# A hybrid SSD and attention block on one core: operands at equal offsets, a later residual, and a head in an order set by hand

## The chip, the cores and the metric

The kernel runs on one core of one Trainium2 chip. The metric is the time of one execution on the device, in microseconds. The core's engines are named as in the profile: PE (matrix products; PEld is its loading of the stationary operand), DVE (vector), ACT (scalar), POOL (general), SP (here the engine whose queue issues the DMAs). SBUF is the on-chip memory with 128 partitions, and PSUM holds the sums of products.

## The reference, cut to what matters

```python
D_MODEL, SEQ, D_FF = 1024, 512, 2816      # one layer, batch 1, float32
def reference(x, ln_in_g, ln_in_b, w_in, ...):
    h = _layernorm(x, ln_in_g, ln_in_b)   # (x - mean) * rsqrt(var + eps) * g + b
    mix = _mixing(h, w_in, ...)           # h @ w_in, cut into the inputs of two branches:
                                          #  SSD (32 heads, chunked scan; y + xs * D_skip),
                                          #  indexer + attention (16 heads over chosen keys),
                                          #  two gates; w_br_ssd, w_br_att, then w_out
    h = _layernorm(DN_ALPHA * h + mix, ln1_g, ln1_b)
    f = _conv_ffn(h, ffn_w_up, ffn_conv_w, ffn_conv_b, ffn_w_down)
    return _layernorm(DN_ALPHA * h + f, ln2_g, ln2_b)
```

What matters here is the first line (the normalized input, called the **head** of the kernel with the first small projections), and that h comes back later as the residual `DN_ALPHA * h`.

## The kernel before, in words

Nearly every product is made in three parts: a float32 matrix is split into a high part (`hi`, a copy rounded by ACT) and a low part (`lo`, the difference, by DVE), and PE adds hi·hi, lo·hi and hi·lo into one PSUM tile (`mm3`, `proj`, `tok_mm`). A weight tile of 128 x 1024 numbers is loaded by SP into a raw buffer `wraw` (pool `wrw`, two buffers), split into `whi` and `wlo` (pool `whl`, three buffers each), and used by 24 products of 128 x 128 by 512 columns (384 for the indexer's queries `w_qi`). `wload` issues these loads ahead of their use, but SP's queue is in order: a load that waits for a raw buffer holds back what stands behind it.

The head: x is loaded as four tiles of 128 tokens. DVE makes mean and variance (`ln_stats`), POOL the inverse root (a power, line 155), and x is normalized in place (tile 1 by ACT, the others by DVE, line 295). PE transposes the tiles into PSUM (line 311), DVE or ACT scales each of the 8 transposed blocks by g and b into `hf` (lines 315 and 317, g and b in the table `pvec`), ACT and DVE split it into `hhi` and `hlo` (`split`). PE then projects `w_small` (104 columns per block of 128 rows), `w_qi[0]` to `w_qi[3]`, and the first large one is `w_ckv`. Meanwhile POOL makes the low parts of the first two weight tiles (line 303) and multiplies the normalized x by g and adds b for the residual, 16 operations of 128 x 512 (lines 327 and 328, g and b spread over the partitions in `gB` and `bB`); the result goes to DRAM (`htok_d`, line 330) and is read back late (line 906). `prow` is a table of row vectors spread over the partitions. `Dv` holds the SSD's D_skip, 64 x 16 numbers for each half of the partitions, loaded by two DMAs at line 482.

After the head come the xbc and z projections and the scan, `w_br_ssd`, the attention heads one by one (`tm` is the mask with the position bias, made by POOL at line 763 and read by DVE at line 774, then the key-value products), `w_br_att`, `w_out`, the second normalization, `w_up` and `w_down`. PE runs in one order written out by the program in the middle part; elsewhere a scheduler decides by priorities.

SBUF tiles come from two sides: pools of weights, `hhi`/`hlo` and others from the left, and the pool `wk` (activations, gates, keys and so on) from the right. In the built program the left tiles that PE reads begin at 128 modulo 512 bytes, those of the right at 480, and `ckhi`/`cklo` at 160, because the small tile `m8` of 32 bytes lies ahead of them. An operand of the right beside one of the left thus begins 32 bytes off, modulo 64. In the program 1057 of the 4053 products of 512 columns have a stationary and a moving operand that differ in this way: all those of `w_br_ssd` (384, names `yhi`, `ylo`), of `w_br_att` (192, `yahi`, `yalo`), and of `w_down` and `w_out` where one operand is of the right, besides the keys' and values' from `ckn`.

Of the kernel before, what the change touches and what calls it, by code (L numbers as in the profile page):

```python
# [67 lines left out]
def block_kernel(ctx, tc, A, out):  # L68
# [215 lines left out]
    raws = [wrw.tile([P, D], F32, name="wraw", tag="wraw") for _ in range(2)]
    nc.sync.dma_start(raws[0][:, :KD * 104], A["w_small"])
    nc.sync.dma_start(raws[1], A["w_qi"][0])
    stats = [ln_stats(t, i) for i, t in enumerate(xt)]
    for i, (t, (mv, rs)) in enumerate(zip(xt, stats)):
        if i == 1:
            nm = st([P, 1], "nm")  # L290
            nc.vector.tensor_scalar(nm, mv[:, 0:1], -1.0, None, OP.mult)
            nc.scalar.activation(t, t, AF.Identity, bias=nm)
            nc.scalar.activation(t, t, AF.Copy, scale=rs)
        else:
            nc.vector.tensor_scalar(t, t, mv[:, 0:1], rs, OP.subtract, OP.mult)
# [810 lines left out]
```

## Time and profile before

| what | us |
|---|---|
| median of three runs | 1142.55 (1140.33 to 1143.06) |
| the profiled execution's own time | 1140.93 |
| its span, from the first to the last instruction | 1139.2 |
| PE busy | 1104.3 |
| DVE, ACT, POOL busy | 806.7, 442.8, 184.3 |

The profile is of one execution. An engine's busy time is to be set against the span; what an idle stretch of PE ended with, and in which stretch it lies, is read from the waits, the windows and the timelines below. The granted clock is the share of TensorE's 2.4 GHz that the throttle let through: 1.00 is 2.4 GHz, 0.50 is 1.2 GHz.

### The profile page before, as it was taken

What the parts mean: (1) busy time and instruction counts of PE and PEld (TensorE: products, weight loads), DVE (VectorE), ACT (ScalarE), POOL (GpSimd) and SP (SyncE); (2) the same over time, 40 slices, a digit from 0 to 9 for tenths busy, and PEclk for the clock granted to TensorE, in tenths of its full rate; (3) what the DMA queues carried; (4) which work ended last, traced back from release to release, by engine and by line L of the source; (5) the groups of instructions that cost most, each with busy time, mean ns of one, the idle gap of its engine ahead of it and who ended that gap; (6) DMA issues with size and microseconds to landing.
All of it is one profiled execution on the core that took longest, in us unless ns stands there. A gap on an engine that the chain in (4) does not pass through costs nothing.

```text
span 1139.2 us, 14494 instructions
## 1 busy us (share of the span) xinstructions
PE 1104.3 (97%) x5394; PEld 902.7 (79%) x5394; DVE 806.7 (71%) x1536; ACT 442.8 (39%) x694; POOL 184.3 (16%) x179
## 2 busy tenths in 40 slices
PE   4799999999999999999999999999999999999996
PEld 3688888887888888878778778889888888888885
DVE  7479798876789899958998936586665566642227
ACT  3355344434333232335645523314444444432120
POOL 7600023312113122012323300040000000000002
PEclk9899999999999999999999999999999999999999
DMA  4452133363323322322211224622223222222241
GB/s 154 149 188 87 63 140 122 126 215 112 120 102 130 130 93 75 129 97 71 88 70 66 83 84 157 225 90 74 93 94 107 96 93 93 101 103 93 93 129 74
DMA packets 43718, 125.58 MB, mean 110 GB/s; under 512 B 6801, under 2 KB 11201, under 8 KB 43649
## 3 DMA queue, kind: packets, MB, share of 16 engines
q1 hardware_dynamic: 43648, 124.67, 31.4%
q8 instruction: 42, 0.69, 0.2%
q14 instruction: 28, 0.22, 0.1%
HBM read 118.20 MB, written 9.59 MB: 112 GB/s over the span
## 4 chain that ended last, share of the span: by engine, by line
PE 73%; DVE 2%; issue 0%; DMA 0%; ACT 0%; POOL 0%; DVEq 0%; SPq 0%; ACTq 0%; POOLq 0%
PE pacc L200 42%; PE pacc L224 5%; PE pc L200 5%; PE ptr L224 4%; PE pa L200 3%; PE pb L200 3%; PE pb L224 2%; PE pc L224 2%; PE pa L224 2%; PE ptr L200 2%; PE pb L203 1%; PE pc L580 1%; PE pa L203 1%; PE pb L576 0%; DMA G<-ac_d 0%
## 5 line engine op out<-in xcount | busy, mean ns | idle before, releaser
L174 DVE TENSOR_TENSOR wlo<-wraw,whi 128x1024 fp32r<-128x1024 f32 x161 | 205.2, 1275 | 165.6 <-ACT whi L173 165.2
L173 ACT ACTIVATE whi<-wraw 128x1024 fp32r<-128x1024 f32 x161 | 170.5, 1059 | 280.9 <-PE pacc L200 163.9
L200 PE MATMUL pacc<-hhi,whi 128*128 128x512 f32 (+1 forms) x552 | 223.7, 405 | 10.7 <-ACT whi L173 10.7
L200 PE MATMUL pacc<-hlo,whi 128*128 128x512 f32 (+2 forms) x552 | 217.2, 394 | 1.4 <-DVE hlo L160 1.4
L200 PE MATMUL pacc<-hhi,wlo 128*128 128x512 f32 (+2 forms) x552 | 215.8, 392 | 0.0
L200 PEld LDWEIGHTS pacc<-hhi,whi 128*128 128x128 f32 (+1 forms) x552 | 104.2, 189 | 33.6 <-ACT whi L173 11.2
L200 PEld LDWEIGHTS pacc<-hlo,whi 128*128 128x128 f32 (+1 forms) x552 | 104.1, 189 | 24.6 <-DVE hlo L160 2.2
L200 PEld LDWEIGHTS pacc<-hhi,wlo 128*128 128x128 f32 (+1 forms) x552 | 104.0, 189 | 18.1
L155 POOL TENSOR_TENSOR rs_y<-rs_v,mhalf 128x1 f32<-128x1 f32 (+1 forms) x18 | 17.1, 954 | 504.3 <-DVE rs_v L153 501.7
L200 PE MATMUL pacc<-h1hi,wlo 128*128 128x512 f32 (+1 forms) x216 | 79.0, 366 | 0.0
L200 PE MATMUL pacc<-h1hi,whi 128*128 128x512 f32 (+1 forms) x216 | 78.9, 366 | 0.0
L200 PE MATMUL pacc<-h1lo,whi 128*128 128x512 f32 (+1 forms) x216 | 78.7, 366 | 0.0
L763 POOL TENSOR_TENSOR tm<-mask,toe 128x128 f32<-128x128 f32 (+1 forms) x64 | 45.6, 715 | 166.2 <-DVE mn L774 102.7
L585 POOL TENSOR_TENSOR v<-v,eaB 128x384 f32<-128x384 f32 x16 | 23.7, 1483 | 238.1 <-DVE eaB L583 147.1
L497 DVE SCALAR_TENSOR_TENSOR cv<-pacc,cwb,cv 128x511 f32<-128x511 f32 (+2 forms) x72 | 53.3, 741 | 0.4
L200 PE MATMUL pacc<-yhi,whi 128*128 128x512 f32 x128 | 51.8, 406 | 0.1
L200 PE MATMUL pacc<-ylo,whi 128*128 128x512 f32 x128 | 51.1, 399 | 0.0
L200 PE MATMUL pacc<-yhi,wlo 128*128 128x512 f32 x128 | 50.6, 395 | 0.0
L777 ACT ACTIVATE l<-l,mn 128x128 f32<-128x128 f32 (+1 forms) x64 | 35.7, 559 | 33.5 <-DVE mn L774 31.9
L200 PEld LDWEIGHTS pacc<-h1hi,whi 128*128 128x128 f32 x216 | 40.7, 189 | 6.7
L200 PEld LDWEIGHTS pacc<-h1hi,wlo 128*128 128x128 f32 x216 | 40.8, 189 | 6.6
L200 PEld LDWEIGHTS pacc<-h1lo,whi 128*128 128x128 f32 x216 | 40.5, 188 | 6.5
(460 smaller groups left out, 2250.7 us busy)
## 6 DMA issues: line engine op xcount, KB each, us to landing
wraw<-in_w_up_dram SPq DMA_DIRECT2D x44, 512.0 KB, 3.4
wraw<-in_w_xbc_dram SPq DMA_DIRECT2D x24, 512.0 KB, 3.5
wraw<-in_w_down_dram SPq DMA_DIRECT2D x22, 512.0 KB, 3.4
G<-ac_d SPq DMA_DIRECT2D x16, 512.0 KB, 4.4
wraw<-in_w_z_dram SPq DMA_DIRECT2D x16, 512.0 KB, 3.5
wraw<-in_w_br_ssd_dram SPq DMA_DIRECT2D x16, 512.0 KB, 3.5
eaB<-ea_d SPq DMA_DIRECT2D x32, 128.0 KB, 3.2
wraw<-in_w_ga_dram SPq DMA_DIRECT2D x8, 512.0 KB, 3.5
```

The source lines that it names most:

```text
L155: last_pow[0] = nc.gpsimd.tensor_tensor(y, v, mhalf[:, :n], OP.pow)
L173: nc.scalar.activation(hi[:, :cols], raw[:, :cols], AF.Copy)
L174: nc.vector.tensor_tensor(lo[:, :cols], raw[:, :cols], hi[:, :cols].bitcast(F32), OP.subtract)
L200: pe(nc.tensor.matmul(p, a, b, start=start, stop=stop).ins)
L203: pe(nc.tensor.transpose(p, a, b).ins)
L224: nc.tensor.matmul(p, x[a][:, tok(i)], w[b][h], start=first and j == 0, stop=last and j == 2)
L497: nc.vector.scalar_tensor_tensor(y[:, d:], p[:, :T - d], cwb[:, 24 * k + c:24 * k + c + 1], y[:, d:], OP.mult, OP.add)
L580: nc.tensor.matmul(yd[h * 64:(h + 1) * 64, tok(c)], xd[:, c, h], G[:, h, c], start=True, stop=True)
L585: nc.gpsimd.tensor_tensor(v[:, P:], v[:, P:], eaB[:, P:], OP.add)
L763: nc.gpsimd.tensor_tensor(tm[:, :K - f], maskt[i][:, f:], self.toe[:, 2 * P - K + f:], OP.add)
L777: nc.scalar.activation(l[:, :K], l[:, :K], AF.Exp, bias=self.mn[:, ic], scale=-1.0, accum_out=self.sm[:, ic])
```

## The change

1. **The start of SP's queue.** Four raw buffers instead of two. `w_small`, `pvec`, three `w_qi` tiles and `prow` are loaded right behind x. D_skip has become a part of `prow`; the two DMAs of `Dv` are gone, and two DVE copies take it out of `prow`.
2. **The head.** All statistics and the normalization of tiles 2 and 3 are on DVE, tiles 0 and 1 on ACT, in an order set by `put` (each instruction after the one before it on its engine). POOL does the four powers only. The low parts of the first weight tiles move from POOL to DVE, behind the eight `hlo`. PE first does 8 products on tiles 1 and 2 of x as they come, whose results are overwritten; then the transposes, then the hi parts of the weights with both parts of h for `w_small`, `w_qi[0]` and `w_qi[1]`, pair by pair of blocks, and last the products with the weights' low parts. `w_qi[2]` follows from the fourth raw buffer.
3. **The residual.** The normalized x goes to `htok_d` without g and b. The 16 POOL operations stand behind the read back (lines 928 and 929 of the kernel after), before `w_out`, with `lig` and `lib` in place of `gB` and `bB`.
4. **Offsets.** A tile of 88 numbers on the right side and `m8` behind `cklo`. In the built program the left tiles and `ckhi`/`cklo` then begin at 192 modulo 512 bytes and those of the right at 128. Of 4053 products 12 differ modulo 64; 978 still differ modulo 512, by 64 bytes.
5. **Kl.** The low part of the keys is two tiles (pools `e2` and `kl`) in place of one.

```diff
+PAD = 88
...
+ROWS = [("dt_bias", NH), ("A_log", NH), ("idx_g", 64), ("idx_b", 64), ("D", NH)]
...
-    wrw = E(tc.tile_pool(name="wrw", bufs=2))
+    wrw = E(tc.tile_pool(name="wrw", bufs=4))
...
+
+    pad = E(tc.tile_pool(name="pad", bufs=1, side="right"))
+    pad.tile([P, PAD], F32, name="pad")
     wk = E(tc.tile_pool(name="wk", bufs=1, side="right"))
...
+    raws = [wrw.tile([P, D], F32, name="wraw", tag="wraw") for _ in range(4)]
+    nc.sync.dma_start(raws[0][:, :KD * 104], A["w_small"])
     voff, vn = _offsets(VECS)
     pvec = ct([P, vn], "pvec")
     nc.sync.dma_start(pvec, A["pvec"])
     vec = {n: pvec[:, s] for n, s in voff.items()}
-
+    for j in range(3):
+        nc.sync.dma_start(raws[1 + j], A["w_qi"][j])
+    roff, rn = _offsets(ROWS)
+    prow = wt("m2", [P, rn], "prow")
+    nc.sync.dma_start(prow, bcast(A["prow"], rn))
+    row = {n: prow[:, s] for n, s in roff.items()}
+
+    Dv = ct([P, NH // 2], "Dv")
     ones = ct([P, P], "ones")
...
-    wq = []
-    for j, raw in enumerate(raws):
...
+    def put(eng, i):
+        if eng in line:
+            tc.add_manual_dep(i.ins, line[eng].name, NOSYNC, reason="order")
+        line[eng] = i.ins
...
+            put(V, nc.vector.bn_stats(s[:, j], t[:, half_of(j)]))
+        mv = st([P, 2], f"x_mv{i}")
...
+    wcols = [slice(0, KD * 104)] + [slice(0, D)] * 3
+
+    def w_hi(j):
+        put(S, nc.scalar.activation(wq[j][0][:, wcols[j]], raws[j][:, wcols[j]], AF.Copy))
+
+    def w_lo(j):
+        c = wcols[j]
+        put(V, nc.vector.tensor_tensor(wq[j][1][:, c], raws[j][:, c], wq[j][0][:, c].bitcast(F32), OP.subtract))
+
+    chain[0] = True
+    trs = [acc_tile() for _ in range(3)] + [tr_tile() for _ in range(2)] + [ps(t) for t in "abc"]
+    for i, n in ((1, 6), (2, 2)):
+        for _ in range(n):
+            mm(trs[7][:, :P], ident, xt[i][:, :P], start=True, stop=True)
+    for i, t in enumerate(xt):
...
+                put(V, nc.vector.tensor_scalar(x_, x_, mvs[i][:, 0:1], rss[i], OP.subtract, OP.mult))
+            for k in range(4 * j, 4 * j + 4):
+                mm_t(trs[k][:, tok(i)], t[:, tok(k)], ident)
+        nc.sync.dma_start(htok_d[:, i], t)
+    w_hi(0)
+    hfs = [wt("v", [P, T], "hf") for _ in range(2)]
...
-            nc.vector.tensor_scalar(hf, tr, g_, b_, OP.mult, OP.add)
-        split(hhi[:, k], hlo[:, k], hf)
-
-
-    for j in range(2):
-        gB, bB = [wt("m2", [P, T], n) for n in ("gB", "bB")]
-        nc.sync.dma_start(gB, bcast(A["ln_in_g"][half_of(j)], T))
-        nc.sync.dma_start(bB, bcast(A["ln_in_b"][half_of(j)], T))
-        for i in range(NT):
-            xh = xt[i][:, half_of(j)]
-            nc.gpsimd.tensor_tensor(xh, xh, gB, OP.mult)
-            nc.gpsimd.tensor_tensor(xh, xh, bB, OP.add)
-            if j == 1:
-                nc.sync.dma_start(htok_d[:, i], xt[i])
-
-
+            put(V, nc.vector.tensor_scalar(hfs[k], trs[k], g_, b_, OP.mult, OP.add))
+
+    for k in range(0, KD, 2):
+        evict(k)
+        evict(k + 1)
+        for j in (k, k + 1):
+            put(S, nc.scalar.activation(hhi[:, j], hfs[j], AF.Copy))
+            put(V, nc.vector.tensor_tensor(hlo[:, j], hfs[j], hhi[:, j].bitcast(F32), OP.subtract))
+        if k < 6:
+            w_hi(1 + k // 2)
+    for j in range(4):
+        w_lo(j)
+
+
+    accs = [acc_tile() for _ in range(3)]
     hTq = [(a[:, P:], b[:, P:]) for a, b in hT]
     TQ = T - P
...
+        p, w, m, r = first[j]
+        for k in ks:
+            for x_ in r[k]:
+                mm(p, w[0][:, k * m:(k + 1) * m], x_, start=k == 0 and x_ is r[k][0], stop=False)
+
+    his(0, (0, 1))
+    his(1, (0, 1))
+    for k in range(2, KD, 2):
+        his(0, (k, k + 1))
+        his(1, (k, k + 1))
+        his(2, (k - 2, k - 1))
+    his(2, (6, 7))
+    for p, w, m, r in first:
         for k in range(KD):
-            mm3(accs[j][:, :TQ], wq[j], tok(k), hTq[k], k == 0, k == KD - 1)
-    roff, rn = _offsets(ROWS)
-    prow = wt("m2", [P, rn], "prow")
-    nc.sync.dma_start(prow, bcast(A["prow"], rn))
-    row = {n: prow[:, s] for n, s in roff.items()}
+            mm(p, w[1][:, k * m:(k + 1) * m], r[k][0], start=False, stop=k == KD - 1)
+    chain[0] = False
+    for b in range(2):
+        hs = slice(b * 64, (b + 1) * 64)
+        nc.vector.tensor_copy(Dv[hs], row["D"][hs].rearrange("p (q b) -> p b q", b=2)[:, b])
     smallT = wt("m2", [104, T], "smallT")
     nc.scalar.activation(smallT, accs[0][:104], AF.Copy)
...
+        proj(p[:, :TQ], wq[3] if j == 2 else w_("w_qi", j), hTq)
         stack_parts(qi[2 * j], qi[2 * j + 1], p, 1.0, slice(0, TQ))
...
-    Dv = ct([P, NH // 2], "Dv")
-    Da = A["ssd_D"]
-    for b in range(2):
-        nc.sync.dma_start(Dv[b * 64:(b + 1) * 64],
-                          bass.AP(tensor=Da.tensor, offset=Da.offset + b, ap=[[0, 64], [2, NH // 2]]))
-
...
         Kh = wt("k4", [P, 2, T], "Kh", F32R)
-        Kl = wt("kl", [P, 2, T], "Kl", F32R)
+        Kl = [wt(t, [P, T], "Kl", F32R) for t in ("e2", "kl")]
         for hh, b in ((0, 0), (1, 64)):
             hs, os_ = slice(b, b + 64), slice(64 - b, P - b)
             nc.scalar.activation(Kh[hs, hh], p[hs], AF.Copy)
-            nc.gpsimd.memset(Kl[os_, hh].bitcast(F32), 0.0)
-            nc.vector.tensor_tensor(Kl[hs, hh], p[hs], Kh[hs, hh].bitcast(F32), OP.subtract)
+            nc.gpsimd.memset(Kl[hh][os_].bitcast(F32), 0.0)
+            nc.vector.tensor_tensor(Kl[hh][hs], p[hs], Kh[hs, hh].bitcast(F32), OP.subtract)
             nc.vector.tensor_copy(Kh[os_, hh], Kh[hs, hh].bitcast(F32))
...
 
+    h1 = [wt("k4" if i < 2 else "g4", [P, D], "h1") for i in range(NT)]
+    lir = {(n, j): wt("m2" if j else "e2", [P, T], "li" + n) for j in range(2) for n in "gb"}
+    with tc.issue_after(last_w[0].ins):
+        for (n, j), t in lir.items():
+            nc.sync.dma_start(t, bcast(A["ln_in_" + n][half_of(j)], T))
+        for i in range(NT):
+            nc.sync.dma_start(h1[i], htok_d[:, i])
+    for i in range(NT):
+        for j in range(2):
+            t = h1[i][:, half_of(j)]
+            nc.gpsimd.tensor_tensor(t, t, lir["g", j], OP.mult)
+            nc.gpsimd.tensor_tensor(t, t, lir["b", j], OP.add)
+
+
```


**SP at the start**, before. The names: `wraw` is a raw buffer, `htok_d` the residual in DRAM.

```order
L128 DMA pvec<-in_pvec_dram 128x346
L285 DMA wraw<-in_w_small_dram 128x832
L286 DMA wraw<-in_w_qi_dram 128x1024
L323 DMA gB<-in_ln_in_g_dram 128x512
L324 DMA bB<-in_ln_in_b_dram 128x512
L323 DMA gB<-in_ln_in_g_dram 128x512
L324 DMA bB<-in_ln_in_b_dram 128x512
L342 DMA prow<-in_prow_dram 128x192
L482 DMA Dv<-in_ssd_D_dram 64x16x1 x2
L167 DMA wraw<-in_w_qi_dram 128x1024 x3
L167 DMA wraw<-in_w_ckv_dram 128x1024 x2
L330 DMA htok_d<-x 128x1024 x3
```

And now:

```order
L135 DMA wraw<-in_w_small_dram 128x832
L138 DMA pvec<-in_pvec_dram 128x346
L141 DMA wraw<-in_w_qi_dram 128x1024 x3
L144 DMA prow<-in_prow_dram 128x224
L353 DMA htok_d<-x 128x1024 x4
L184 DMA wraw<-in_w_qi_dram 128x1024
L184 DMA wraw<-in_w_ckv_dram 128x1024 x2
```

The `w_qi` loads stand ahead of `prow`, `Dv` and the broadcasts of g and b are gone from here, and the residual's writes follow at once.

**DVE in the head**, before (`hf` is the scaled transposed block, `hlo` its low part, `wlo` a weight's):

```order
L295 TENSOR_SCALAR x<-x,ln_mv_157,rs_y_3_161 128x1024
L317 TENSOR_SCALAR hf<-ptr,pvec 128x512
L317 TENSOR_SCALAR hf<-pa,pvec 128x512
L317 TENSOR_SCALAR hf<-pc,pvec 128x512
L160 TENSOR_TENSOR hlo<-hf,hhi 128x512 x2
L317 TENSOR_SCALAR hf<-ptr,pvec 128x512
L160 TENSOR_TENSOR hlo<-hf,hhi 128x512
L317 TENSOR_SCALAR hf<-pa,pvec 128x512
L160 TENSOR_TENSOR hlo<-hf,hhi 128x512 x2
L174 TENSOR_TENSOR wlo<-wraw,whi 128x1024
L160 TENSOR_TENSOR hlo<-hf,hhi 128x512 x3
L174 TENSOR_TENSOR wlo<-wraw,whi 128x1024 x2
```

And now:

```order
L350 TENSOR_SCALAR x<-x,x_mv_175,x_y_178 128x512 x2
L364 TENSOR_SCALAR hf<-pacc,pvec 128x512
L402 COPY Dv<-prow 64x16 x2
L371 TENSOR_TENSOR hlo<-hf,hhi 128x512 x2
L364 TENSOR_SCALAR hf<-pacc,pvec 128x512
L371 TENSOR_TENSOR hlo<-hf,hhi 128x512 x2
L364 TENSOR_SCALAR hf<-ptr,pvec 128x512
L371 TENSOR_TENSOR hlo<-hf,hhi 128x512 x2
L364 TENSOR_SCALAR hf<-pb,pvec 128x512
L364 TENSOR_SCALAR hf<-pc,pvec 128x512
L371 TENSOR_TENSOR hlo<-hf,hhi 128x512 x2
L336 TENSOR_TENSOR wlo<-wraw,whi 128x832
```

The copies into `Dv` have come in behind the first `hf`, and the weight tiles' low parts stand behind all eight `hlo`.

**POOL at the last attention head**, before (`tm` is mask plus bias of one block of queries, the number behind `mask` the block):

```order
L763 TENSOR_TENSOR tm<-mask_114,toe 128x256
L763 TENSOR_TENSOR tm<-mask_115,toe 128x256
L763 TENSOR_TENSOR tm<-mask_112,toe 128x128
L763 TENSOR_TENSOR tm<-mask_113,toe 128x256
L763 TENSOR_TENSOR tm<-mask_114,toe 128x256
L763 TENSOR_TENSOR tm<-mask_115,toe 128x256
L155 TENSOR_TENSOR rs_y_0_6631<-rs_v_0_6629,mhalf 128x1
L920 TENSOR_TENSOR h_6570<-h_6570,l1g 128x512
L921 TENSOR_TENSOR h_6570<-h_6570,l1b 128x512
```

And now (`h_6141` to `h_6144` are the four tiles of the residual):

```order
L816 TENSOR_TENSOR tm<-mask_129,toe 128x256
L816 TENSOR_TENSOR tm<-mask_130,toe 128x256
L928 TENSOR_TENSOR h_6141<-h_6141,lig 128x512
L928 TENSOR_TENSOR h_6143<-h_6143,lig 128x512
L816 TENSOR_TENSOR tm<-mask_127,toe 128x128
L816 TENSOR_TENSOR tm<-mask_128,toe 128x256
L929 TENSOR_TENSOR h_6141<-h_6141,lib 128x512
L929 TENSOR_TENSOR h_6143<-h_6143,lib 128x512
L816 TENSOR_TENSOR tm<-mask_129,toe 128x256
L816 TENSOR_TENSOR tm<-mask_130,toe 128x256
L928 TENSOR_TENSOR h_6142<-h_6142,lig 128x512
L929 TENSOR_TENSOR h_6142<-h_6142,lib 128x512
```

Two multiplications stand ahead of the last head's first `tm`, and two additions between its second and its third; the other operations follow.

## Rows read from the trace of the kernel before

**Rows 1.** The page's engine row: busy us, share of the span, instructions.

```profile
PE 1104.3 (97%) x5394; PEld 902.7 (79%) x5394; DVE 806.7 (71%) x1536; ACT 442.8 (39%) x694; POOL 184.3 (16%) x179
```

**Rows 2.** PE's waits in the whole span: us in total, times, longest us.

```profile
PE ptr L311 <- DVE x L295: 11.2, 2, 10.2
PE pacc L200 <- ACT whi L173: 10.7, 1, 10.7
```

**Rows 3.** SP's timeline, 9 to 39 us: start us, us, instruction.

```profile
9.31 0.33 SPq L342 DMA_DIRECT2D prow<-in_prow_dram  x1
9.75 1.85 SPq L482 DMA_DIRECT2D Dv<-in_ssd_D_dram  x2
14.98 23.64 SPq L167 DMA_DIRECT2D wraw<-in_w_qi_dram  x3
```

**Rows 4.** Issue to landing, from the views of the tiles Dv and prow.

```profile
DMA to landing us min/median/max: 13.9/18.7/23.4
...
DMA to landing us min/median/max: 5.8/5.8/5.8
```

**Rows 5.** DMA view, 14.9 to 31 us.

```profile
DMA packets 1647, 0.01 MB, mean 0 GB/s; under 512 B 1647, under 2 KB 1647, under 8 KB 1647
```

**Rows 6.** Windows: PE, PEld, DVE, ACT, POOL busy; clock share; DMA share; GB/s.

```profile
10.20:25.90 15.70, 12.86 (x54) 9.65 (x54) 14.66 (x20) 8.00 (x12) 14.50 (x11) 1.00 0.30 83
25.90:36.60 10.70, 0.00 (x2) 0.00 (x1) 1.63 (x2) 1.11 (x2) 10.70 (x9) 0.66 0.27 98
```

**Rows 7.** PE's timeline before the stall and at the first w_ckv product.

```profile
24.99 0.39 PE L200 MATMUL pacc<-hhi,wlo 128*104 128x512 f32 x1
25.22 0.34 PE L200 MATMUL pacc<-hlo,whi 128*128 128x384 f32 x1
25.39 0.34 PE L200 MATMUL pacc<-hhi,whi 128*128 128x384 f32 x1
...
56.23 0.39 PE L200 MATMUL pacc<-hhi,whi 128*128 128x512 f32 x1
```

**Rows 8.** POOL and DVE in the head: ns min/median/max, first to last start us.

```profile
L327 POOL TENSOR_TENSOR x<-x,gB x8: 1258/1494/1732, 14.9 to 31.0; 128x512 f32<-128x512 f32 x8
L328 POOL TENSOR_TENSOR x<-x,bB x8: 1258/1276/2257, 23.6 to 45.2; 128x512 f32<-128x512 f32 x8
...
L160 DVE TENSOR_TENSOR hlo<-hf,hhi x8: 679/1400/2465, 18.3 to 40.5; 128x512 fp32r<-128x512 f32 x8
```

**Rows 9.** Lines, 0 to 50 us, then the page: busy us, mean ns | idle before.

```profile
L159 ACT ACTIVATE hhi<-hf 128x512 fp32r<-128x512 f32 x8 | 4.5, 620 | 0.0
L315 ACT ACTIVATE hf<-ptr,pvec 128x512 f32<-128x512 f32 x2 | 1.5, 773 | 2.7 <-PE ptr L311 2.7
...
L174 DVE TENSOR_TENSOR wlo<-wraw,whi 128x1024 fp32r<-128x1024 f32 x161 | 205.2, 1275 | 165.6 <-ACT whi L173 165.2
L173 ACT ACTIVATE whi<-wraw 128x1024 fp32r<-128x1024 f32 x161 | 170.5, 1059 | 280.9 <-PE pacc L200 163.9
```

**Rows 10.** The chain of waits, 675 to 1130 us: start, us, engine, tile, instructions.

```profile
678.70 41.67 PE pacc L200 x178
...
1039.36 2.04 PE pacc L224 x9
...
1061.55 2.11 PE pacc L224 x9
```

**Rows 11.** POOL, DVE and PE at the last two heads, from their timelines.

```profile
649.13 0.39 PE L200 MATMUL ptr<-Kl,Q 128*128 128x512 f32 x1
...
652.36 1.42 POOL L763 TENSOR_TENSOR tm<-mask,toe 128x256 f32<-128x256 f32 x2 [3.65 <-DVE mn L774]
...
660.56 0.48 DVE L774 CUSTOM_DVE_ANT_0 l<-ptr,tm,mf 128x256 f32<-128x256 f32 x1
```

**Rows 12.** Issue to landing of the late h loads.

```profile
DMA to landing us min/median/max: 5.6/6.8/8.5
```

**Rows 13.** Windows, columns as in group 6: the stretch of w_br_att.

```profile
684.00:727.00 43.00, 43.00 (x185) 34.55 (x184) 27.98 (x35) 15.44 (x19) 0.00 (x0) 1.00 0.45 159
```

More of the change, by code (lines that the diff above doesn't have):

```diff
@@ L281, in block_kernel @@
     dt, dts, acT, cd = [kp.tile(SH, F32, name=n, tag=n) for n in ("dt", "dts", "acT", "cd")]
[L284 to L295, printed above, removed]
@@ L296, in block_kernel @@
-    wq = []
-    for j, raw in enumerate(raws):
-        hi = whl.tile([P, D], F32R, name="whi", tag="whi")
-        lo = whl.tile([P, D], F32R, name="wlo", tag="wlo")
-        cols = slice(0, D if j else KD * 104)
-        nc.scalar.activation(hi[:, cols], raw[:, cols], AF.Copy)
-        with tc.issue_after(last_pow[0].ins):
-            nc.gpsimd.tensor_tensor(lo[:, cols], raw[:, cols], hi[:, cols].bitcast(F32), OP.subtract)
-        wq.append((hi, lo))
-    wq.append(w_("w_qi", 1, ahead=0))
@@ L306, in block_kernel @@
-    accs = [acc_tile() for _ in range(3)]
-    trs = ["tr", "tr", "a", "b", "c", "tr", "tr", "a"]
-    for k in range(KD):
-        tr = tr_tile() if trs[k] == "tr" else ps(trs[k])
-        for i in range(NT):
-            nc.tensor.transpose(tr[:, tok(i)], xt[i][:, tok(k)], ident)
-        hf = wt("v", [P, T], "hf")
+    m8 = kp.tile([P, 8], F32, name="m8")
+    nc.scalar.activation(st([P, 1], "warm"), ones[:, :1], AF.Copy)
+    line = {}
+    def put(eng, i):
+        if eng in line:
+            tc.add_manual_dep(i.ins, line[eng].name, NOSYNC, reason="order")
+        line[eng] = i.ins
+        return i
@@ new lines, in block_kernel @@
+    whls = [[whl.tile([P, D], F32R, name=n, tag=n) for n in ("whi", "wlo")] for _ in range(2)]
+    y8s = [flat(wt("y8", [P, 4, T], "wq", F32R)) for _ in range(2)]
+    wq = [whls[0]] + [[y[:, half_of2(j)] for y in y8s] for j in range(2)] + [whls[1]]
+    wcols = [slice(0, KD * 104)] + [slice(0, D)] * 3
[4 more added lines that the diff above has]
+        put(V, nc.vector.tensor_tensor(wq[j][1][:, c], raws[j][:, c], wq[j][0][:, c].bitcast(F32), OP.subtract))
@@ new lines, in block_kernel @@
+    chain[0] = True
[3 more added lines that the diff above has]
+            mm(trs[7][:, :P], ident, xt[i][:, :P], start=True, stop=True)
+    for i, t in enumerate(xt):
+        if i < 2:
+            put(S, nc.scalar.activation(t, t, AF.Identity, bias=nms[i]))
+            put(S, nc.scalar.activation(t, t, AF.Copy, scale=rss[i]))
+        for j in range(2):
+            x_ = t[:, half_of(j)]
+            if i > 1:
+                put(V, nc.vector.tensor_scalar(x_, x_, mvs[i][:, 0:1], rss[i], OP.subtract, OP.mult))
+            for k in range(4 * j, 4 * j + 4):
+                mm_t(trs[k][:, tok(i)], t[:, tok(k)], ident)
+        nc.sync.dma_start(htok_d[:, i], t)
@@ L333, in block_kernel @@
+    for k in range(0, KD, 2):
[9 more added lines that the diff above has]
+    accs = [acc_tile() for _ in range(3)]
     hTq = [(a[:, P:], b[:, P:]) for a, b in hT]
     TQ = T - P
-    for k in range(KD):
-        mm3(accs[0][:104], wq[0], slice(k * 104, (k + 1) * 104), hT[k], k == 0, k == KD - 1)
@@ L901, in block_kernel @@
         wo[k] = w_halves("w_out", k)
-    h1 = [wt("k4" if i < 2 else "g4", [P, D], "h1") for i in range(NT)]
     l1r = {(n, j): wt("v", [P, T], "l1" + n) for j in range(2) for n in "gb"}
     with tc.issue_after(last_w[0].ins):
-        for i in range(NT):
-            nc.sync.dma_start(h1[i], htok_d[:, i])
         for (n, j), t in l1r.items():
```

32 lines of the change are left out of this document (22 added, 10 removed).

## The prediction, as it was put on record

> **What bounds the kernel now.** I read the engine row first: PE is busy for 1104.3 us of a span of 1139.2 [rows 1]. So the time is the sum of PE's products plus about 35 us in which PE stands. Two things can be gained: idle time of PE, and the duration of a product. PE's waits [rows 2] put the idle time in the head: two waits for the normalized x, 10.2 us of them the start, when nothing has been loaded yet, and one of 10.7 us for the high part of a weight tile. All other waits of PE are under 1 us each.
>
> The queue of SP tells where the 10.7 us come from [rows 3]. The second `w_qi` tile is issued at 14.98, behind the two DMAs of `Dv`, issued from 9.75 on. These took 13.9 and 23.4 us to land [rows 4]. The DMA view of the time behind that issue shows 1647 packets that carry 0.01 MB in all, each under 512 bytes [rows 5]: single numbers of 4 bytes, with a weight tile of 512 KB behind them. In the windows [rows 6] the reader sees two stretches: from 10.2 to 25.9 PE works 12.86 of 15.7 us at the full clock of 2.4 GHz (1.00), with DVE and POOL busy for nearly all of it; from 25.9 to 36.6 PE does nothing, and the granted clock is 0.66 on average, so part of the stretch is at 1.2 GHz. The head's end, for my sum, is the first product of `w_ckv`, at 56.23 [rows 7].
>
> The second thing is read from the chain of waits further on [rows 10]: 178 products of `w_br_att` take 41.67 us, 234.1 ns each. In `w_down`, one and the same line takes 2.04 us for nine products at 1039 (226.7 ns each) and 2.11 at 1061 (234.4). The operands differ only in where they begin: in the slow groups one is of the left side and one of the right, 32 bytes apart modulo 64.
>
> **The head, part by part.** Without the `Dv` DMAs no weight tile waits for them. All raw tiles of the head but `w_qi[3]` are issued ahead of `prow`, and that one behind the residual's writes, which are large packets. The new wait is DVE's: the copies into `Dv` stand behind the first `hf` and wait for `prow`. Behind them all `hlo` are queued, and PE waits for these. Before, `prow` was issued at 9.31 behind about as many bytes and took 5.8 us [rows 3, 4]: I let DVE go on at 15.2.
>
> From there DVE and ACT work alternately. ACT's share is eight `hhi` at 0.62, three `hf` at 0.77 and three weight tiles at 1.06 [rows 9], 5.0 + 2.3 + 3.2 = 10.5 us, of which about 1 us lies ahead of 15.2. DVE's is less, if its `hlo` take the 0.68 us of the row's minimum: their median of 1.40 and maximum of 2.47 [rows 8] stand in a time in which POOL multiplied x by g, and that work is gone from here. So the last `hlo` ends at 15.2 + 9.5 = 24.7, and four low parts of weights follow, at most 1.28 each [rows 9], the last by 29.8.
>
> PE's work in the head is 24 products of `w_small` at 0.23 and 96 of `w_qi` at 0.17 [rows 7]: 5.5 + 16.3 = 21.8 us. The products of the high weights end some 2.3 us behind the last `hlo`, at 27.0; those of the low weights take 8 x 0.23 + 16 x 0.17 = 4.6 and end at 31.6; `w_qi[2]` and `w_qi[3]` take 4.1 each, to 39.8. The first `w_ckv` product then comes at about 40.3, with half a microsecond for a hand-over. That is **15.9 us earlier**. The bounds: if PE never waits from 15.2 on, 37.0 (19.2 earlier); if the eight `hlo` stay at 1.40 in spite of the idle POOL, 8 x 0.72 = 5.8 later than I take it, 46.1 (10.1 earlier). I take 15.9, since 0.68 is what the row itself shows as its fastest case. The eight products on raw x cost nothing: they lie in time in which PE waits for x anyway. If that cover were gone, they would cost under 1 us (eight of 128 columns, by the 0.17 of 384).
>
> **The offsets.** Some 1045 products change from 32 bytes apart to equal modulo 64. At 7.4 to 7.7 ns each [rows 10] that is **7.8 us**, if equality modulo 64 is what counts, and PE sets the pace where they lie: in `w_br_att`'s stretch it does, with PE busy for 43.0 of 43 us and DVE for 28 [rows 13]. But all fast rows of before have operands that are equal modulo 512 as well, and 978 of the changed products stay 64 bytes apart there. So the bounds are 0 and 7.8. I take 7.8, because the slow rows differ by 32 bytes and the new distance is a multiple of twice that, but I hold it for little better than even.
>
> A rule speaks against this term as a whole. The Trainium skill ("SBUF — State Buffer", section "Who interferes with whom") says that only the port pair of DVE and GpSimd causes contention and that PE's reads of the moving operand and of the weights are independent. By that rule the term would be 0 and the sum 7.8 us higher. The trace doesn't agree with it here: one line shows 226.7 and 234.4 ns with nothing but the operands' places changed [rows 10].
>
> **The later residual.** Sixteen operations of POOL, 8 x 1.49 + 8 x 1.28 = 22.2 us by their medians [rows 8], now stand in the last heads and `w_br_att`. Queued behind the first four are the last head's `tm`, for which DVE and then PE wait. The two additions need `lib`, whose buffer is free when PE has read the keys of head 14, at 649.5 [rows 11]. With a landing of up to 8.5 us [rows 12] that is 658; two additions of 1.26 to 2.26 [rows 8] end at 660.5 to 662.5, and the third and fourth `tm`, made at 652.36 before, come by 664 at the latest. DVE first wants the third at 660.56 [rows 11]. So up to 3.4 us late, most likely within 1. Then about 18 us of POOL's work lie beside DVE in `w_br_att`. DVE has 15 us free in 43 [rows 13]; if each POOL operation shut it out wholly, it would need 28 + 22 = 50 us, 7 more than PE. I charge **0.7 us** for both, with bounds 0 and 7.
>
> The two-part `Kl`, the third and fourth raw buffer and the earlier writes of x cost nothing: same instructions, loads that start sooner, and a queue with large packets. Their cover is that PE's waits behind the head are under 1 us each already.
>
> **The sum.** 1140.93 - 15.9 - 7.8 + 0.7 = 1117.9 for the profiled execution. The median of the runs lies 1.6 us above that execution, so I forecast 1119.5, rounded to 1119.
>
> **The rivals.**
> A (my forecast): head and offsets pay. With PE never waiting in the head 1116, with a part of C's waits 1123.
> B: the change doesn't do what its offsets say, because 64 bytes apart modulo 512 is still unequal. For it: no row of before shows this distance at 512 columns with 128 rows of weights. Time: 1119.5 + 7.8 = 1127.3.
> C: the head keeps a wait. `prow` is the new gate of DVE; if it lands 13.9 us after its issue, as the faster `Dv` DMA did [rows 4], everything behind slides by 8.1: 1127.6. If `hlo` stays slow, 5.8: 1125.3. If the residual shuts DVE out, 6.3: 1125.8. With unpaid offsets up to 1135. Against it: `prow` has 128 long rows, not single numbers.
> D, slower than before: the clock. PE now works between many short waits for `hlo`, and if the throttle grants 1.2 GHz from 15.2 to the head's end, the 21.8 us of products become 43.6. PE's waits of about 3 us are filled, so the head ends at 40.3 + 19 = 59.3, 3.1 later than before. With unpaid offsets the time is 1142.55 + 3.1 + 0.7 = 1146.4, with paid ones 1138.6. It decides when more than 15 us of such extra time arise and the offsets give nothing. Against it: 12.86 of 15.7 us busy kept 1.00, and the clock fell only where PE did nothing [rows 6].
>
> **How the numbers follow.** A 0.48, B 0.28, C 0.19, D 0.05. A measurement of this kernel can tell about 0.3% (3.4 us) from no change. A, B and nearly all of C are faster than that: 0.92. D with paid offsets and C's worst end lie within it: 0.04; D without them is slower: 0.04. The range goes from 1113, A's good end and 2 to 3 us for PE's small waits behind the head, which the two further raw buffers may end, to 1131, which takes in B with its bounds and most of C; beyond lie C with unpaid offsets and D, some 0.14, and below 1113 some 0.05.
>
> **What would show it.** In the profile after: PE's waits without one for `whi` of 10 us; the first `w_ckv` product at 38 to 43; `hlo` near 0.68 us with POOL idle beside it; the clock at 1.00 from 15 on; `w_br_att`'s 178 products in 40.4 us and nine of `w_down` always in 2.04. I am wrong on the offsets if `w_br_ssd` and `w_br_att` still take 234 ns each, on the head if DVE waits for `prow` beyond 16 us or the first `w_ckv` product comes behind 46, and on the residual if PE waits for the last head's `l` or `pt` by more than 1 us, or DVE's two-input operations in `w_br_att`'s stretch are as long as the head's `hlo` were.

## The result: 1128.8 us, and where the 13 us come from

The changed kernel takes 1128.82 us in the median of four runs (1127.05 to 1129.85), beside 1141.88 for the kernel before on the same chips. The ratio is 0.9887, with a 95% interval from 0.9875 to 0.9900: 1.1% faster, clear of the noise. The forecast was 1119, with a range of 1113 to 1131. The time lies in the range, at the place of rival B (1127.3), and not at the forecast.

Two lines of the page of after, and the waits of PE that bear on what follows (whole span; us in total, times, longest us), answer to [rows 1, 2]:

```profile
span 1126.3 us, 14551 instructions
...
PE 1102.1 (98%) x5410; PEld 902.7 (80%) x5410; DVE 804.2 (71%) x1542; ACT 443.0 (39%) x697; POOL 177.6 (16%) x177
...
PE pc L217 <- DMA x<-in_x_dram: 5.7, 1, 5.7
PE pacc L217 <- DVE cv L550: 2.5, 2, 2.0
PE pa L259 <- ACT cks L519: 1.6, 1, 1.6
PE pb L629 <- DVE pv L617: 1.2, 1, 1.2
...
PE pa L220 <- DVE l L841: 0.8, 1, 0.8
...
PE pc L506 <- DVE acT L504: 0.5, 1, 0.5
```

The wait of 10.7 us is gone. PE's busy time has hardly moved (1104.3 to 1102.1), but it now holds 3.76 us of the eight products on raw x and a stretch at half clock, so it doesn't tell what the offsets gave; the chains further down do. New waits have come for `cks` (ACT's squares of the `w_ckv` products), `acT` (the decays) and `l` (the attention weights), and one of 2.0 us for `cv` (the convolution, at 175.7). That one lies between two rows of the table below between which the lead still grows by 0.6.

The best account of a kernel with one long chain of products is the moment at which the same product starts in both traces:

| product | before | after | lead |
|---|---|---|---|
| first of `w_ckv` | 56.23 | 40.23 | 16.0 |
| first transpose of the scan (`ident,xs`) | 109.17 | 97.11 | 12.1 |
| first of `w_br_ssd` | 234.40 | 221.71 | 12.7 |
| last of `w_br_ssd` | 497.79 | 484.56 | 13.2 |
| first of the attention heads' transposes (`ident,l`) | 515.74 | 502.33 | 13.4 |
| first of `w_br_att` | 666.45 | 655.02 | 11.4 |
| first of `w_down` with `fw` | 1046.90 | 1035.36 | 11.5 |
| last product | 1130.02 | 1117.16 | 12.9 |

So 16.0 us were won in the head, 3.9 were lost between it and the scan, 1.3 came back by the attention heads, 2.0 were lost in the last two heads, and 1.3 were won in `w_down`.

**The head** is as forecast. The issue of `prow` by SP and its landing, DVE's timeline, the eight `hlo`, and PE's first `w_ckv` product, all of after (these answer to [rows 3, 4, 7, 8]):

```profile
5.59 0.33 SPq L144 DMA_DIRECT2D prow<-in_prow_dram  x1
...
DMA to landing us min/median/max: 9.1/9.1/9.1
...
13.30 0.81 DVE L364 TENSOR_SCALAR hf<-pacc,pvec 128x512 f32<-128x512 f32 x1
14.72 0.40 DVE L402 COPY Dv<-prow 64x16 f32<-64x16 f32 x2 [0.60 <-DMA prow<-in_prow_dram]
15.14 1.29 DVE L371 TENSOR_TENSOR hlo<-hf,hhi 128x512 fp32r<-128x512 f32 x2
...
L371 DVE TENSOR_TENSOR hlo<-hf,hhi x8: 684/692/693, 15.1 to 24.0; 128x512 fp32r<-128x512 f32 x8
...
40.23 0.47 PE L217 MATMUL pacc<-hhi,whi 128*128 128x512 f32 x1
```

`prow` is what DVE waits for, and the eight `hlo` take 0.69 us each, against up to 2.47 before. POOL is not idle beside them, though the prediction took it to be: a power on 128 x 32 numbers runs there from 14.83 to 20.27, and it slows neither the `hlo` nor the copies (0.2 each).

**The loss behind the head** is in PE's timeline of after (start, us, product, idle time before it and its releaser) and in the windows beside it (columns as in [rows 6]):

```profile
59.32 0.46 PE L506 MATMUL pc<-acT,lastrow 128*128 128x128 f32 x2 [0.47 <-DVE acT L504]
61.34 0.38 PE L259 MATMUL pa<-ones,cks 128*128 128x1 f32 x2 [1.56 <-ACT cks L519]
...
63.11 0.63 PE L217 MATMUL pacc<-hlo,whi 128*128 128x512 f32 x1
63.53 0.63 PE L217 MATMUL pacc<-hhi,whi 128*128 128x512 f32 x1
...
57.50:61.60 4.10, 2.06 (x13) 1.36 (x12) 2.19 (x4) 3.75 (x7) 0.00 (x0) 1.00 0.20 67
62.60:65.70 3.10, 3.10 (x9) 2.34 (x8) 2.33 (x10) 0.90 (x2) 0.00 (x0) 0.50 0.99 383
```

PE stands for 0.47 and 1.56 us, and right behind it the clock is granted at 0.50: seven products start 0.43 us apart instead of 0.23, some 1.5 us more. The sum is 3.5 of the 3.9 lost.

**The loss in the last heads**, from POOL's, DVE's and PE's timelines of after:

```profile
633.18 2.81 POOL L928 TENSOR_TENSOR h<-h,lig 128x512 f32<-128x512 f32 x2 [1.14 <-PE pa L220]
...
640.43 2.53 POOL L929 TENSOR_TENSOR h<-h,lib 128x512 f32<-128x512 f32 x2 [1.89 <-DMA lib<-in_ln_in_b_dram]
...
634.71 2.37 DVE L191 TENSOR_TENSOR wlo<-wraw,whi 128x1024 fp32r<-128x1024 f32 x1
...
641.52 3.29 DVE L841 TENSOR_SCALAR l<-l,rc 128x128 f32<-128x128 f32 x4
...
638.55 3.31 PE L217 MATMUL pc<-pt,V 128*64 128x512 f32 x16
...
652.84 0.30 PE L220 MATMUL pa<-ident,l 128*128 128x128 f32 x1 [0.83 <-DVE l L841]
```

Of before, the same groups of DVE and PE:

```profile
648.14 1.64 DVE L174 TENSOR_TENSOR wlo<-wraw,whi 128x1024 fp32r<-128x1024 f32 x1
...
653.97 1.27 DVE L788 TENSOR_SCALAR l<-l,rc 128x128 f32<-128x128 f32 x4
...
651.98 2.38 PE L200 MATMUL pc<-pt,V 128*64 128x512 f32 x16
```

The loss has two parts. The sixteen products of `pt` and `V` take 0.93 longer; they lie ahead of the scalings of `l`, and the late operation in front of them is DVE's `wlo`, 2.37 instead of 1.64 us while POOL multiplies by `lig` and makes `tm`. Then DVE's four scalings of `l` (`l<-l,rc`) take 3.29 instead of 1.27 us while POOL adds `lib`, and in the last head PE waits 0.83 for `l`. Which of DVE's slowed operations costs how much was not tried one by one.

**The offsets** in the chain of waits of after, to be set against [rows 10]: `w_br_att`, then nine products of `w_down` with an operand of the left, and with one of the right:

```profile
667.27 41.66 PE pacc L217 x178
...
1033.26 2.04 PE pacc L241 x9
...
1055.26 2.06 PE pacc L241 x9
```

`w_br_att` is as slow as before (41.66 against 41.67). `w_down` has gained most of its 7 ns per product, 2.06 against 2.11.

### The profile page after: what moved, and what is told of

Read it like the earlier page. It is cut to its first block, busy times and chain, and to the rows that moved or that the text cites. A ratio compares the mean times of both kernels' runs of the same rounds, so it can differ in the third digit from the quotient of the medians.

```text
span 1126.3 us, 14551 instructions
## 1 busy us (share of the span) xinstructions
PE 1102.1 (98%) x5410; PEld 902.7 (80%) x5410; DVE 804.2 (71%) x1542; ACT 443.0 (39%) x697; POOL 177.6 (16%) x177
## 4 chain that ended last, share of the span: by engine, by line
PE 91%; DMA 3%; DVE 3%; ACT 1%; issue 1%; SPq 0%; DVEq 0%; ACTq 0%
PE pacc L217 56%; PE pc L217 5%; PE pacc L241 5%; PE ptr L241 4%; PE pa L217 3%; PE pb L217 3%; DMA G<-ac_d 2%; PE pc L241 2%; PE pb L241 2%; PE pa L241 2%; PE ptr L217 2%; PE pc L633 1%; PE pb L629 1%; PE pa L610 1%; PE pb L220 1%; DMA prow<-in_prow_dram 1%
## 5 line engine op out<-in xcount | busy, mean ns | idle before, releaser
L191 DVE TENSOR_TENSOR wlo<-wraw,whi 128x1024 fp32r<-128x1024 f32 x159 | 201.5, 1267 | 158.1 <-ACT whi L190 158.1
L190 ACT ACTIVATE whi<-wraw 128x1024 fp32r<-128x1024 f32 x159 | 168.2, 1058 | 265.2 <-PE pacc L217 175.2
L217 PE MATMUL pacc<-hhi,whi 128*128 128x512 f32 (+1 forms) x536 | 218.8, 408 | 3.5 <-DVE cv L550 2.5
L217 PE MATMUL pacc<-hlo,whi 128*128 128x512 f32 (+1 forms) x536 | 212.2, 396 | 0.8 <-DVE hlo L371 0.8
L217 PE MATMUL pacc<-hhi,wlo 128*128 128x512 f32 (+1 forms) x536 | 210.3, 395 | 0.0
L217 PEld LDWEIGHTS pacc<-hhi,whi 128*128 128x128 f32 (+1 forms) x536 | 101.2, 189 | 26.5 <-issue 4.2
L217 PEld LDWEIGHTS pacc<-hlo,whi 128*128 128x128 f32 (+1 forms) x536 | 100.9, 188 | 25.3 <-DVE hlo L371 3.6
L217 PEld LDWEIGHTS pacc<-hhi,wlo 128*128 128x128 f32 (+1 forms) x536 | 101.1, 189 | 19.1 <-issue 1.0
L172 POOL TENSOR_TENSOR rs_y<-rs_v,mhalf 128x1 f32<-128x1 f32 (+1 forms) x14 | 14.0, 1000 | 469.6 <-DVE rs_v L170 468.6
```

What stands on the lines that cost most here:

```text
L172: last_pow[0] = nc.gpsimd.tensor_tensor(y, v, mhalf[:, :n], OP.pow)
L190: nc.scalar.activation(hi[:, :cols], raw[:, :cols], AF.Copy)
L191: nc.vector.tensor_tensor(lo[:, :cols], raw[:, :cols], hi[:, :cols].bitcast(F32), OP.subtract)
L217: pe(nc.tensor.matmul(p, a, b, start=start, stop=stop).ins)
```

## The experiments: offsets

Three kernels move operands only. In the first two the kernel before gets `m8` behind `cklo` and a pad on the right side; its left side begins at 128 modulo 512, so a pad of 104 numbers gives the distance of after (64 bytes), and one of 88 gives equality.

```diff
-    m8 = kp.tile([P, 8], F32, name="m8")
...
+    m8 = kp.tile([P, 8], F32, name="m8")      # behind ckhi, cklo, dt ...
+    pad = E(tc.tile_pool(name="pad", bufs=1, side="right"))
+    pad.tile([P, 104], F32, name="pad")       # second kernel: 88; ahead of the pool wk
```

> The kernel before with only the offsets of the kernel after (m8 moved behind cklo, a pad of 104 numbers, so that left and right operands lie 64 bytes apart modulo 512, as after). Theory 1 (equality modulo 64 counts, the forecast's term): 7.8 us less than before, about 1134, w_br_att's products at 227 ns. Theory 2 (equality modulo 512 counts, and the sign of the distance matters, as the trace of after suggests): products whose moving operand is of the right and lies behind the weights' offset stay at 233 to 234 ns, those the other way round go to about 230, so 1.5 to 2.5 us less, about 1140.

Measured: 1139.91 us, ratio 0.9985 (0.9977 to 0.9994), 1.5 us less than before.

> The kernel before with m8 moved and a pad of 88 numbers, which here makes left and right operands equal modulo 512 (4019 of 4053 products). Theory 2: all these products at 227 ns, 7 to 8 us less than before, about 1134 to 1135. Theory 1 expects the same here, and the same as with 64 bytes apart. Rival 3 (the offsets are a symptom, the lengths come from DVE or from the tiles themselves): no change, 1142.

Measured: 1134.76 us, ratio 0.9943 (0.9930 to 0.9956), 6.7 us less. The third kernel is the kernel after with `PAD = 72`.

> The kernel after with a pad of 72 numbers in place of 88: left and right operands equal modulo 512. Theory 2: 5.5 to 6.5 us less than after, about 1123, and w_br_ssd, w_br_att and w_down at 227 ns. Theory 1 and rival 3: no change, 1129.

Measured: 1125.33 us, ratio to before 0.9861 (0.9846 to 0.9876), 3.5 us less than after. The chains of waits, `w_br_att` in the three kernels in this order:

```profile
677.76 41.66 PE pacc L202 x178
...
676.36 40.57 PE pacc L202 x178
...
666.40 40.57 PE pacc L217 x178
```

With operands 64 bytes apart, `w_br_att` keeps its 234 ns; with operands equal modulo 512 it has 227.9, in the kernel before as in the kernel after. So theory 2 holds against theory 1: equality modulo 64 is not enough, equality modulo 512 is; between the first two kernels nothing but the pad's size differs. Distances of 128 or 256 bytes were not run, so a rule modulo 128 or 256 would fit as well. What 64 bytes cost is not the same everywhere: in `w_br_att` the moving operand is of the right side, at 128, and the weights at 192, and the 7 ns stay; in `w_down` it is the other way round, and there they cost about 2 ns. But the sign of the distance alone doesn't decide it, as theory 2 took it to: in `w_out` the moving `whi` lies 64 bytes ahead of `mhi` and `mlo` as in `w_down`, and 13 such products of after, from 708.77 to 711.80, still start 233 ns apart.

The full gain in time is 6.7 (5.0 to 8.0 by the interval). In the trace of the second kernel the lead grows by 1.75 us over the 384 products of `w_br_ssd` where 2.7 were to be expected; 0.3 of the rest is a longer wait for `pv` in the scan (1.2 for 0.9), the remainder was not followed.

The third kernel gained less than was expected, 3.5 for 5.5 to 6.5. In its trace the clock is granted at 0.50 from 175.1 to 178.5, behind a wait of 2.0 us for `cv` that after has too, with 1.00 behind it: where its lead over after had been 0.9, it is 0.6 behind. Then comes a wait of 2.0 us for a table of the position bias, at 227.2, that after had for 0.2.

## The experiments: what the head's 16 us are made of

The kernel before, with D_skip as a part of `prow` and nothing else:

```diff
-        nc.sync.dma_start(Dv[b * 64:(b + 1) * 64], ...)
+        nc.vector.tensor_copy(Dv[hs], row["D"][hs].rearrange("p (q b) -> p b q", b=2)[:, b])
```

> The kernel before with D_skip taken from prow by two DVE copies, so that only the two small DMAs are gone. Theory (they alone cause the 10.7 us stall and the 1.5 us at half clock behind it): 11 to 12.5 us less than before, about 1130. Rival (another wait stands right behind: two raw buffers, w_qi low parts on POOL, hlo slowed): 5 us less or fewer.

Measured: 1134.68 us, ratio 0.9941 (0.9927 to 0.9956), 7.1 less. Neither number came, 11 to 12.5 or 5 and fewer: the first `w_ckv` product came 7.7 us earlier, not 12. PE's longest wait behind the start, a window behind that wait, and `hlo`:

```profile
PE pacc L200 <- DVE hlo L160: 2.9, 1, 2.9
...
25.90:31.00 5.10, 5.10 (x21) 4.58 (x20) 5.10 (x5) 0.93 (x2) 5.10 (x4) 0.69 0.00 0
...
L160 DVE TENSOR_TENSOR hlo<-hf,hhi x8: 1041/1759/1780, 20.9 to 34.9; 128x512 fp32r<-128x512 f32 x8
```

The stall gives way to the next one: `hlo` at 1.76 us in the median (1.40 before), with POOL busy for all of the 5.1 us, and the clock at 0.50 until 29.1. The rival had the right mechanism.

```diff
-            nc.gpsimd.tensor_tensor(xh, xh, gB, OP.mult)
-            nc.gpsimd.tensor_tensor(xh, xh, bB, OP.add)
```

> As the run before it, and the 16 multiplications and additions of POOL in the head are left out (the residual lacks g and b). Theory (POOL's reads slow hlo from 0.68 to 1.40 us, and hlo paces PE in the head): hlo near 0.7 us and 3 to 6 us less than with the DMAs alone gone, about 1125 to 1127. Rival (hlo is slow for another reason or paces nothing): within 1 us.

Measured: 1126.33 us, ratio 0.9872 (0.9855 to 0.9888), 8.4 us less than with the DMAs alone gone, more than the 3 to 6 expected, and 15.4 less than before. The first line is `hlo`, the second the first `w_ckv` product:

```profile
L160 DVE TENSOR_TENSOR hlo<-hf,hhi x8: 678/681/691, 18.0 to 23.7; 128x512 fp32r<-128x512 f32 x8
...
41.31 0.39 PE L200 MATMUL pacc<-hhi,whi 128*128 128x512 f32 x1
```

Two edits of a few lines, with two raw buffers and the old order, bring the first `w_ckv` product to 41.31. The order by hand with its third and fourth buffer adds 1.1 us to that, and 1.0 of it is the eight products on raw x: without them (a run below) the product is at 41.24. The two causes in the head are the small DMAs (7.7) and POOL's multiplications and additions beside DVE (7.2), each with the half clock that came behind its waits.

The same with the residual made late, behind the third load of `w_br_att`, so that nothing is left out:

```diff
+        if n == 2:      # in the loop over w_br_att: loads of h1, lig, lib, then
...
+            nc.gpsimd.tensor_tensor(t, t, lir["g", j], OP.mult)   # and the additions
```

> The kernel before with D_skip from prow and the residual's 16 operations moved behind the third w_br_att load, nothing else: two raw buffers, the old order of the head, the old offsets. Theory (the two causes in the head are the small DMAs and POOL's reads; the order by hand adds little): as the run without these operations, 1126 to 1128, no slower than the whole change. Rival (the order by hand carries a third or more): 1131 or more.

Measured: 1131.75 us, ratio 0.9919 (0.9905 to 0.9932). This is 5.4 us more than without the operations, so the rival's number came, but not for the rival's reason:

```profile
12.13 4.92 POOL L303 TENSOR_TENSOR wlo<-wraw,whi 128x832 fp32r<-128x832 f32 x2
...
14.77 2.31 DVE L474 COPY Dv<-prow 64x16 f32<-64x16 f32 x1
...
45.05 0.39 PE L200 MATMUL pacc<-hhi,whi 128*128 128x512 f32 x1
...
PE ptr L928 <- DVE h L925: 0.9, 1, 0.9
PE ptr L928 <- POOL h L922: 0.7, 1, 0.7
```

The copies into `Dv` slipped ahead of the first `hf`, and one of them, of 64 x 16 numbers, took 2.31 us and ended with POOL's low parts of two weight tiles (0.2 in after). PE waits 2.0 us for that `hf`. Then its products start 0.43 us apart until 24, where they lay 0.23 apart in the run before it: the trace's first record of the clock, at 1.00, begins at 24.3, there at 18.4. Together they put the first `w_ckv` product at 45.05. Two more are lost in `w_out`, where DVE and POOL come late for PE. So what the order by hand is worth beyond the two causes is not settled by this run: it fixes where such copies stand.

> The run before it with m8 behind cklo and a pad of 88 numbers, which makes operands equal modulo 512 here. If effects add: 6.7 us less, 1119.5 to 1121.5, faster than both kernels.

Measured: 1124.97 us, ratio 0.9856 (0.9841 to 0.9871): 6.8 us less than the run before it, as the offsets alone gave (6.7). These two effects add; the time named is missed with the run before it.

The kernel after without the 8 products on raw x:

```diff
-    for i, n in ((1, 6), (2, 2)):
-        for _ in range(n):
-            mm(trs[7][:, :P], ident, xt[i][:, :P], start=True, stop=True)
```

> The kernel after without the 8 products on raw x. Forecast's theory: no change within 0.5 us. Rival (they let the transposes run 0.11 us apart instead of 0.21): transposes at 0.21, the first hf and all behind it up to 1.5 us later.

Measured: 1126.80 us, ratio to before 0.9880 (0.9855 to 0.9906), 2.0 us less than after. The rival was right on the head: without them the transposes run 0.21 us apart until 13.0, with them 0.11 from 11.3 on, and the transposes of `smallT` and the first `w_ckv` product come 1.0 us later. These steps stand where each trace's record of the clock begins, at 1.00 (13.1 and 11.3). Ahead of it nothing is recorded, and the 1.00 that a window shows there is no reading. The time did not follow, for a reason of its own: in this trace the clock stayed at 1.00 between 62.6 and 65.7, behind the same waits:

```profile
62.60:65.70 3.10, 3.10 (x16) 2.53 (x16) 2.43 (x8) 1.27 (x4) 0.00 (x0) 1.00 0.93 297
```

## The experiments: the two losses

The transposes of `smallT` and the copy to `smt` written ahead of the last two `w_qi` projections:

```diff
+    tr = v3(tr_tile(), NT, 104)               # moved ahead of: for j in range(2, 4)
+    for i in range(NT):
+        nc.tensor.transpose(tr[:, i], smallT[:, tok(i)], ident[:104, :104])
+    nc.vector.tensor_copy(smt, tr)
```

> The kernel after with the four transposes of smallT and the copy to smt written ahead of the last two w_qi projections. Theory: PE's two new waits near 60 us (0.5 and 1.6 us) and the half clock from 62.6 to 65.7 (1.5 us) come from the chain of DVE and ACT that begins with smt at 40.5 us, only 8 us earlier than before where the w_ckv products are 16 earlier. Then 3 to 4 us less than after, about 1125, no idle time at 59 to 61, and the clock at 1.00 there. Rival (the scheduler's order of PE's instructions or ACT's place for cks is the cause): the waits stay, change within 1 us.

Measured: 1128.53 us, ratio to before 0.9885 (0.9871 to 0.9899), the same as after. The place was right and the sum wrong. Both waits and the half clock near 60 us are gone, and the lead at the first transpose of the scan is 15.9 us instead of 12.1. Then it is given back: 1.5 until the last `w_br_ssd` product, with these two waits, for `pv` in the scan and for the gate `sga` in `w_br_ssd`, and 3.4 from the last heads to `w_down` (2.0 in after), where the clock fell:

```profile
PE pb L629 <- ACT pv L613: 2.0, 1, 2.0
...
PE pacc L217 <- ACT sga L681: 0.7, 1, 0.7
...
652.00:656.00 4.00, 3.58 (x13) 2.72 (x14) 3.63 (x6) 0.41 (x1) 3.13 (x2) 0.69 1.01 381
```

For the last heads, first the 16 operations ordered behind the last `tm`:

```diff
+            with tc.issue_after(last_tm[0].ins):
                 nc.gpsimd.tensor_tensor(t, t, lir["g", j], OP.mult)
...
```

> The kernel after with the 16 residual operations of POOL ordered behind the last attention head's tm. Theory (they hold back tm, and slow DVE's operations beside them, in the last two heads): the 1.9 us that PE lost between 642 and 660 come back, about 1127. Rival (DVE is slowed beside POOL wherever the 16 operations stand): the loss moves into w_br_att's stretch, change within 0.7 us.

Measured: 1130.25 us, ratio to before 0.9899 (0.9883 to 0.9915): 1.4 more than after instead of 1.9 less. Four operations of POOL now lie in a row beside the scaling of `l`, and the clock fell behind PE's waits:

```profile
640.64 5.24 DVE L841 TENSOR_SCALAR l<-l,rc 128x128 f32<-128x128 f32 x4
...
656.00:660.00 4.00, 4.00 (x13) 3.10 (x12) 1.84 (x2) 0.00 (x0) 3.84 (x4) 0.57 1.07 394
```

So `tm` was not the trouble. Then the loads and operations behind the sixth load of `w_br_att`, out of the heads:

```diff
+        if n == 5:      # in the loop over w_br_att: the loads and the 16 operations
```

> The kernel after with the loads and the 16 POOL operations of the residual ordered behind the sixth w_br_att load, so that they run beside w_br_att's products and not beside the last two heads. Theory (POOL's reads slow DVE's scaling of l by 1/sum in the last two heads, 3.3 us for four instead of 1.3, and PE waits for it): the 1.9 us lost between 640 and 660 come back, about 1127, with those four operations at 1.3 us. Rival (the operations cost the same wherever they stand): within 0.7 us of after, with the loss in w_br_att.

Measured: 1126.49 us, ratio to before 0.9869 (0.9853 to 0.9886), 2.3 less than after. The lead at the first `ident,l` and at the first `w_br_att` product is the same, 15.5 us: nothing is lost in the heads, and nothing in `w_br_att`. Most of the rest of the profile's gain (span 1122.3) is again the clock, 1.00 behind the same two waits:

```profile
57.50:61.60 4.10, 2.07 (x13) 1.39 (x12) 2.23 (x4) 3.75 (x7) 0.00 (x0) 1.00 0.21 55
...
62.60:63.60 1.00, 1.00 (x6) 0.83 (x5) 0.55 (x1) 0.30 (x2) 0.00 (x0) 1.00 0.91 307
```

All three together, late residual, early `smallT` and `PAD = 72`:

> The run before it, with smallT transposed early and the pad of 72 numbers (equal modulo 512). If the three effects add: 1128.8 - 1.9 - 0.3 to 3.6 - 3.5 to 5.2, so 1118 to 1123. If the waits of the scan, which took back what the early smallT gave, take it again, 1123.

Measured: 1122.90 us, ratio to before 0.9838 (0.9824 to 0.9851), 5.9 us less than after and the fastest of all. The scan took part of it again: a wait of 2.9 us for `pv` stands in its trace, with the clock at 0.50 behind it from 244.7 to 248.1 and a wait of 1.0 for `sga` later, and the lead falls from 16.1 at the scan's first transpose to 14.4 at the last `w_br_ssd` product.

## Why the prediction was right, and where it was wrong

**The head: right, in size and by its steps.** First `w_ckv` product at 40.3 forecast, 40.23 measured; DVE let go by `prow` at 15.2, measured 14.7; `hlo` at 0.68, measured 0.69; the high weights' products ending at 27.0, measured 27.15; those of the low weights at 31.6, measured 31.77. The experiments confirm both causes and show that the first alone would not have done: without the small DMAs, `hlo` beside POOL becomes the bound. (The second alone was not run.) One term was put at nothing and paid: the eight products on raw x bring 1.0 us.

**The offsets: the failed step is the choice of 7.8 between the ends 0 and 7.8.** I took the multiple of 64 for enough, on the ground that the slow rows differed by 32. All fast rows were equal modulo 512 as well, as the text said, and that stricter property is the one that the runs bear out. Measured: 1.5 for the distance of 64, 6.7 for equality modulo 512. This is rival B with a remainder of a fifth of the term, most of it in `w_down` (1.3). The rule of the Trainium skill that was weighed there ("SBUF — State Buffer", section "Who interferes with whom") would have given 0, near what came, but not for its reason: PE's two reads are not indifferent to each other, since the place of one operand alone moves a product from 234 to 228 ns.

**The residual: the term was mis-sized and its mechanism wrong.** It was priced at 0.7 by way of a late `tm`. The `tm` were in time; DVE's own work beside POOL was not (`wlo` at 2.4 us instead of 1.6, the scaling of `l` at 3.3 instead of 1.3), and PE lost 2.0. Moving the operations out of the heads gave it back, and moving them only behind `tm` made it worse. The same section of the Trainium skill says that `tensor_scalar` can enter a mode that contends with GpSimd, and the rows agree (1.27 alone, 3.29 and 5.24 beside POOL); my text looked at two-input operations in `w_br_att` instead, where nothing was lost.

**What was left out: what is late next behind the head.** The sum let the head's gain run to the end. But `smallT`, from which the index keys and the decays are made, came only 7.8 us earlier where PE came 16 earlier, because its projection now ends with the low weights' products and its transposes stood behind the last `w_qi`. PE arrived at `acT`, and at `cks`, which stands behind that chain on ACT, before they were there: 3.5 us, of which 1.5 are the clock. A row for the start of that chain, compared with the first `w_ckv` product, would have pointed to it before the run.

**Why the time still lay in the range.** For the profiled execution the sum was 1117.9 and the time 1128.35. Of the 10.4 between them 6.5 are the offsets, 1.3 the residual and 3.9 the stretch behind the head, less 1.3 that came back in the scan. The range held because it took in rival B; that the time lies so close to B's 1127.3 is in part luck, since the 3.9 stood in no rival, and 2.6 came back in `w_down` and in the scan.

**The clock (rival D): not in the head, as argued, but elsewhere.** It stayed at 1.00 from 14.8 to 57. The argument for that was in part misread: the transposes of before lie 0.21 us apart until 19.1, where its record of the clock begins, so the 1.00 of its window from 10.2 to 25.9 [rows 6] is full clock only in the last part.

Behind the head, five kernels have the same waits of 0.5 and 1.6 us near 60, in the same order of instructions: in three the clock fell for 3.4 us (after, the one with `PAD = 72`, the one with `tm` first), in two it did not. Nor does it take such waits: in the kernel before without the residual's operations it fell from 62.7 to 66.2 with no wait of PE near it, behind a stretch of small products (`ones,cks`, one column each), and that trace loses 1.6 of its lead there. Two of the experiments have a fall in the last heads, one at 175, one at 245, at a price of 1 to 2 us each time. The runs of one kernel differ by it as well: without the eight products three runs have a granted clock of 0.997 to 0.998 over the whole span and take 1125.8 to 1127.0 us, the fourth has 0.993 and takes 1132.7. So a microsecond or two between two of these kernels can be the clock alone, and what decides it stays open.

**Open** is what the scan takes back. Between its first transpose and the last `w_br_ssd` product the lead grew by 1.2 us in after, grew by 2.0 in the run without the residual's operations, and fell by 1.5 and 1.6 in the two runs with the early `smallT`, whose waits for `pv` are the longest (2.0 and 2.9). It fell by 1.4 without the small DMAs too, where the waits are for `pv` (1.6) and `sga` (0.8) again. What sets these waits was not tried.

## What to carry to other kernels

When a stall at the start is removed, follow the second chain that starts there too: the step that used to have slack becomes the next wait, and here it took back a fifth of the gain. POOL's operations on whole tiles must not stand beside DVE's work that PE waits for, and pushing them behind one consumer's input can put them beside another's. An offset rule read from fast rows is safe only in the strictest form in which all of them agree: 512 bytes here, where 64 was not enough.
